# Decoder layer: hi and lo parts of two activation forms side by side, one 512-column matmul for two of 256, and reordered bank reads

## The chip, the cores and the metric

The kernel runs on one core of a Trainium2 chip. The metric is device microseconds of one execution: the median of 3 runs before is 844.3 us (843.54 to 844.47). The profiled execution, whose trace is quoted here, took 844.19 us; its span from first to last instruction is 842.4 us.

## The reference

One decoder layer on 512 tokens of width 1024, in float32. The parts that matter here:

```python
def memory_cross_attention(h, m, w_q, w_kv, w_o):
    q = (h @ w_q).reshape(b, s, MEM_HEADS, MEM_HEAD_DIM)
    kv = (m @ w_kv).reshape(b, mlen, 2, MEM_HEADS, MEM_HEAD_DIM)   # m: 256 memory tokens
    k, v = kv[:, :, 0], kv[:, :, 1]
    probs = softmax(einsum('bshd,bmhd->bhsm', q, k) / sqrt(MEM_HEAD_DIM))
    ...
# in reference():
    x = x + merged @ w_mix_out            # after attention, convolution and their merge
    x = x + memory_cross_attention(rms_norm(x, ..), rms_norm(mem, ..), ...)
    hf = rms_norm(x, norm_ffn)
    gate, up = split(hf @ w_ffn_in, 2)    # w_ffn_in: 1024 x 5632
    x = x + (silu(gate) * up) @ w_ffn_out # w_ffn_out: 2816 x 1024
return rms_norm(x, norm_final)
```

## The kernel before

**Two parts of a number.** TensorE takes operands in fp32r. Every operand is therefore split: ScalarE casts it (`hi`), and VectorE subtracts the cast from the original (`lo`, in the code the *rest*). A product is three matmuls, hi x hi, hi x lo and lo x hi, added up in one PSUM bank. A bank holds 512 float32 columns. PSUM has three pools of banks: `pmm` (2 banks), `pz` (4) and `po` (2); a bank is taken again when its last reader is done.

**Memory keys** (`km`). Eight groups, one per 128 key columns. `load_w` fetches the weights (SyncE queue), ScalarE casts them (L151), VectorE makes the rest (L152, `wl`). For each of eight k a 512-column matmul multiplies the weights' hi part with a tile `mgs[k]` that holds hi and lo of the 256 memory tokens side by side, and a 256-column matmul adds the weights' lo part times the tokens' hi part. The two halves of the bank are added afterwards: ScalarE copies the right one (L666), VectorE adds the left one (L667), then multiplies by the tokens' norm (L668) and splits the result. Groups alternate between the two banks of `pmm`. A scheduler sets the order on each engine here; `after(x, earlier)` forces an order on one engine.

**Entry.** `residual` adds the attention's result to the stream, block by block of 128 channels, and `forms_of` turns each pair of an even and an odd channel block (`xe`, `xo`) into seven activation forms of 256 columns, one half of the tokens each.

**Gate and up products.** The hidden width is cut into 22 blocks `m` of 128. For each block the gate and up weights (two column blocks), the even and odd channels and the two halves of the tokens make a 2 x 2 by 2 x 2 block product, done in seven products `i` = 0 to 6 in place of eight (in Strassen's manner). `ffn_form` makes hi and lo of a weight form (cast L872, rest L873, tile `wf`), six products ahead. `product` runs three matmuls for each of four k, 12 matmuls of 256 columns (L883). The order of all products is a list, `uses`, which interleaves block m with block m + 1. Three banks serve a block: `z` (products 0, 3, 4, 5), `v` (product 1) and `y` (products 2 and 6). They are read between products: ScalarE copies z (L904), VectorE reads v after product 1 (L906) and y after product 6 (L909), and `second` reads y after product 2 (L914) before product 6 adds onto it. `evict` multiplies by the norm (L921), applies Silu (ScalarE, L923) and forms the activations (L931, L935). `mean2` and `r2b` work out the norm of the stream during the first blocks: VectorE splits the sums of squares (L196, L197) and two matmuls average them (L202). From here to the end PE, ACT and DVE run in the order in which the code is written (`manual_schedule`).

**The end of these products** prepares the first activation forms (`f01`, `fh`) and weights (`out_cast`, its rest `rest_of`, L964) of the output products (L1152), of which 276 matmuls of 512 columns follow.

Of the kernel before, what the change touches and what calls it, by code (L numbers as in the profile page):

```python
# [44 lines left out]
def hybrid_layer(ctx: ExitStack, tc: tile.TileContext, xT_d, memT_d, mem_d, cols_d, wv_d, win_d,  # L45
# [607 lines left out]
            mem_split(m)  # L653


    km = []
    for m in range(KD):
        w = load_w(wmk_d[m])
        ps = mmtile("km")
        for k in range(KD):  # L660
            nc.tensor.matmul(ps, w[0][:, k, :], mgs[k], start=k == 0, stop=False,
                             skip_group_check=True)
            nc.tensor.matmul(ps[:, :MEM], w[1][:, k, :], mg[k][0], start=False, stop=k == KD - 1,
                             skip_group_check=True)
        t = tmp("km", MEM)
        nc.scalar.copy(t, ps[:, MEM:])  # L666
        nc.vector.tensor_tensor(out=t, in0=ps[:, :MEM], in1=t, op=ALU.add)  # L667
        nc.vector.tensor_tensor(out=t, in0=t, in1=rmb, op=ALU.mult)  # L668
        if m % 2 == 0:
            pair = unit("kmh"), unit("kml")  # L670
        hi, lo = (u[:, (m % 2) * MEM:(m % 2 + 1) * MEM] for u in pair)
        nc.scalar.copy(hi, t)
        nc.vector.tensor_tensor(out=lo, in0=t, in1=f(hi), op=ALU.subtract)
        km.append((hi, lo))
        if m == 0:
            merged.append(split(sig[0], "m"))
    vm = [[None] * 2 for _ in range(MT)]
    for n in range(2):
        pss = [ztile("vm") for _ in range(MT)]
        for c in range(4):  # L680
            w = load_w(wmv_d[n, c], 512)
            for j in range(2):
                k = 2 * c + j
                for t in range(MT):
                    sl = slice(t * P, (t + 1) * P)
                    mm3(pss[t], (mg[k][0][:, sl], mg[k][1][:, sl]),
                        (w[0][:, j, :], w[1][:, j, :]), k == 0, k == KD - 1)
        for t in range(MT):
            vm[t][n] = split(pss[t], "vm", rm[:, t:t + 1])

    def forms_of(xe, xo):

        b11, b12, b21, b22 = xe[:, :HS], xe[:, HS:], xo[:, :HS], xo[:, HS:]
        c, d = f(unit("c1")), f(unit("c2"))
        n1, t3, n2, t4 = c[:, :HS], c[:, HS:], d[:, :HS], d[:, HS:]
        nc.vector.tensor_tensor(out=n1, in0=b11, in1=b12, op=ALU.subtract)
        nc.vector.tensor_tensor(out=t3, in0=b22, in1=b12, op=ALU.subtract)
        nc.vector.scalar_tensor_tensor(out=n2, in0=n1, scalar=-1.0, in1=b22, op0=ALU.mult,  # L700
                                       op1=ALU.subtract)
        nc.vector.scalar_tensor_tensor(out=t4, in0=n2, scalar=-1.0, in1=b21, op0=ALU.mult,
                                       op1=ALU.subtract)
        u = unit("xf")
        nc.scalar.copy(u[:, :HS], b11)
        nc.vector.tensor_tensor(out=u[:, HS:], in0=b11, in1=f(u[:, :HS]), op=ALU.subtract)
        (oh, ol), (ch, cl), (dh, dl) = split(xo, "xo"), split(c, "xc"), split(d, "xd")
        a, b = slice(0, HS), slice(HS, S)
        return [(u[:, a], u[:, b]), (oh[:, a], ol[:, a]), (ch[:, a], cl[:, a]),
                (dh[:, a], dl[:, a]), (ch[:, b], cl[:, b]), (dh[:, b], dl[:, b]),  # L710
                (oh[:, b], ol[:, b])]

    def residual(w_dram, act, old, gain, pairs=False):

# [160 lines left out]

    def product(ps, m, i, ks=range(KP)):

        w = wforms[m, i]
        for k in ks:
            hi, lo = (w[:, j, k * P:(k + 1) * P] for j in range(2))  # L880
            xh, xl = x2f[k][i]
            for j, (a, b) in enumerate(((hi, xh), (hi, xl), (lo, xh))):
                nc.tensor.matmul(ps[:, :HS], a, b, start=i < 3 and k == 0 and j == 0,  # L883
                                 stop=k == KP - 1 and j == 2, skip_group_check=True)

    banks, silus = {}, []
    acts = {}

    def bank_of(m, i):
# [6 lines left out]
            banks[m]["y"] = otile("y")  # L896
        return banks[m]["zvyzzzy"[i]]

    def reads(m, i):

        b = banks[m]
        z, s, t = b["z"][:, :HS], b["s"], b["t"]
        if i in (0, 3, 4):
            nc.scalar.copy((s[:, :HS], None, None, s[:, HS:], t[:, :HS])[i], z)  # L904
        elif i == 1:
            nc.vector.tensor_tensor(out=b["g"][:, :HS], in0=b["v"][:, :HS], in1=s[:, :HS],  # L906
                                    op=ALU.add)
        elif i == 6:
            nc.vector.tensor_tensor(out=b["g"][:, HS:], in0=b["y"][:, :HS], in1=s[:, HS:],  # L909
                                    op=ALU.add)  # L910

    def second(m):
        b = banks[m]
# [165 lines left out]
    with tc.manual_schedule(engines={mybir.EngineType.PE, mybir.EngineType.Activation,  # L1079
# [6 lines left out]
        for n, (m, i) in enumerate(uses):  # L1086
# [3 lines left out]
                product(bank_of(m, i), m, i)  # L1090
            if i == 4:
                reads(m, i)
            else:
                if i == (2 if m == 1 else 1) and m > 0:
                    second(m - 1)
                reads(m, i)
            if n + AHEAD < len(uses):
# [31 lines left out]
            elif (m, i) == (NF - 1, 4):  # L1129
# [5 lines left out]
                rest_of(*x2)  # L1135
                n2_of(x2[0], 0)
        w = out_cast(*w23(1))
        evict(NF - 1, 0)
        evict(NF - 1, 1)
        rest_of(*x3)  # L1140
        rest_of(*w)
        evict(NF - 1, 2)


# [314 lines left out]
```

## Time and profile before

| | |
|---|---|
| Median of 3 runs | 844.3 us |
| Profiled execution | 844.19 us, span 842.4 us |
| TensorE (PE) busy | 833.8 us, 99% |
| Weight loads (PEld) busy | 731.0 us, 87% |
| VectorE (DVE) busy | 658.7 us, 78% |
| ScalarE (ACT) busy | 464.2 us, 55% |
| GpSimd (POOL) busy | 155.6 us, 18% |
| Matmuls | 4694 |

Busy times are shares of one span; the engines work side by side. Matmuls overlap, so a row's duration of a matmul (283 ns for 256 columns) is longer than the step from its start to the next one's. In a row, `out<-in` names the tile written and the tiles read, `L883` is the line of the kernel, and a bracket at the end gives the idle time ahead of the instruction on its engine and what ended it.

### The profile page before, as it was taken

How to read it: one execution, taken by the hardware profiler on the slowest of the kernel's cores; microseconds unless marked ns; L12 is line 12 of the kernel's file. 1: busy time of each engine (PE TensorE's matmuls, PEld its weight loads, DVE VectorE, ACT ScalarE, POOL GpSimd, SP SyncE). 2: the span in 40 equal slices, each digit the busy share in tenths (PEclk: the TensorE clock that was granted, in tenths of full speed). 3: DMA queues.
4: the chain of work that ended last, by engine and by line, in shares of the span. 5: the costliest groups of instructions: out<-in, count | busy, mean ns of one | idle time of the engine just before them, and what ended most of it. 6: DMA issues, size and time to landing. Idle time of an engine off the chain costs nothing.

```text
span 842.4 us, 12559 instructions
## 1 busy us (share of the span) xinstructions
PE 833.8 (99%) x4694; PEld 731.0 (87%) x4694; DVE 658.7 (78%) x1066; ACT 464.2 (55%) x835; POOL 155.6 (18%) x165
## 2 busy tenths in 40 slices
PE   9999999999999999999999999999999999999996
PEld 7888888888888888888888889999999999988885
DVE  7879899986756577586555679888887888899886
ACT  7567878674332255433444557655555555666654
POOL 0011131210666620173000101111111110000401
PEclk9999999999999999999999999999999999999998
DMA  8452454134687865566431425777677772465552
GB/s 301 151 168 102 120 115 114 59 116 172 244 308 269 315 231 189 187 230 238 134 80 51 113 51 153 198 184 190 178 181 194 189 181 85 150 224 202 176 186 101
DMA packets 51359, 143.73 MB, mean 171 GB/s; under 512 B 5761, under 2 KB 7041, under 8 KB 48482
## 3 DMA queue, kind: packets, MB, share of 16 engines
q1 hardware_dynamic: 41650, 107.89, 38.5%
q0 software_dynamic: 9360, 34.75, 15.8%
q8 instruction: 37, 0.61, 0.3%
q10 hardware_dynamic: 288, 0.28, 0.1%
q14 instruction: 24, 0.20, 0.1%
HBM read 125.20 MB, written 13.64 MB: 165 GB/s over the span
## 4 chain that ended last, share of the span: by engine, by line
PE 98%; DMA 1%; DVE 0%; ACT 0%; issue 0%; SPq 0%; DVEq 0%
PE z L883 15%; PE p L1152 12%; PE pr L156 8%; PE pr L157 8%; PE pr L158 8%; PE y L883 8%; PE v L883 4%; PE r L157 3%; PE r L156 3%; PE r L158 3%; PE v L284 2%; PE mq L157 2%; PE mq L158 2%; PE mq L156 2%; PE br L157 2%; PE br L156 2%
## 5 line engine op out<-in xcount | busy, mean ns | idle before, releaser
L151 ACT CAST wh<-wr 128x1024 fp32r<-128x1024 f32 x84 | 88.1, 1051 | 149.4 <-issue 83.7
L152 DVE TENSOR_TENSOR wl<-wr,wh 128x1024 fp32r<-128x1024 f32 x84 | 112.2, 1336 | 37.2 <-ACT wh L151 37.2
L156 PE MATMUL pr<-xgh,wh 128*128 128x512 f32 x288 | 112.8, 392 | 0.0
L157 PE MATMUL pr<-xgl,wh 128*128 128x512 f32 x288 | 112.3, 390 | 0.0
L158 PE MATMUL pr<-xgh,wl 128*128 128x512 f32 x288 | 112.2, 390 | 0.0
L607 POOL TENSOR_TENSOR pre<-pre 128x512 f32<-128x512 f32 x44 | 70.1, 1597 | 32.6 <-DMA pre<-in_w_ffn_out_dram 30.3
L852 POOL DMA_DIRECT2D ws<-in_w_ffn_in_dram x22 | 26.6, 1210 | 256.2 <-DVE wf L873 123.5
L883 PE MATMUL z<-xdh,wf 128*128 128x256 f32 x352 | 70.4, 283 | 0.0
L158 PEld LDWEIGHTS pr<-xgh,wl 128*128 128x128 f32 x288 | 54.1, 188 | 11.6
L156 PEld LDWEIGHTS pr<-xgh,wh 128*128 128x128 f32 x288 | 54.1, 188 | 10.6
L157 PEld LDWEIGHTS pr<-xgl,wh 128*128 128x128 f32 x288 | 54.1, 188 | 10.3
L904 ACT COPY sa<-z 128x256 f32<-128x256 f32 x44 | 16.4, 372 | 81.5 <-PE z L883 81.5
L883 PEld LDWEIGHTS z<-xdh,wf 128*128 128x128 f32 x352 | 58.0, 192 | 0.0
L873 DVE TENSOR_TENSOR wf<-s,wf 128x512 fp32r<-128x512 f32 x44 | 30.4, 690 | 25.7 <-ACT wf L872 25.3
L883 PE MATMUL z<-xdl,wf 128*128 128x256 f32 x176 | 49.8, 283 | 0.0
L964 DVE TENSOR_TENSOR wl<-wr,wh 128x1024 fp32r<-128x1024 f32 x33 | 41.0, 1242 | 4.3 <-ACT wh L1031 4.3
L1031 ACT CAST wh<-wr 128x1024 fp32r<-128x1024 f32 x33 | 34.6, 1050 | 4.4 <-DMA wr<-sums 2.1
L883 PE MATMUL y<-xch,wf 128*128 128x256 f32 x176 | 35.4, 283 | 0.0
L883 PE MATMUL v<-xoh,wf 128*128 128x256 f32 x176 | 35.4, 283 | 0.0
L883 PE MATMUL z<-xf,wf 128*128 128x256 f32 x264 | 35.4, 283 | 0.0
L883 PE MATMUL z<-xch,wf 128*128 128x256 f32 x176 | 35.3, 283 | 0.0
L883 PE MATMUL y<-xoh,wf 128*128 128x256 f32 x176 | 35.3, 283 | 0.0
(350 smaller groups left out, 2377.5 us busy)
## 6 DMA issues: line engine op xcount, KB each, us to landing
wr<-in_w_in_dram SPq DMA_DIRECT2D x36, 512.0 KB, 3.3
pre<-in_w_ffn_out_dram POOLq DMA_DIRECT2D x11, 1024.0 KB, 7.9
sums<-pre POOLq DMA_DIRECT2D x11, 1024.0 KB, 5.1
ws<-in_w_ffn_in_dram SPq DMA_DIRECT2D x22, 512.0 KB, 3.7
wg<-in_w_ffn_in_dram SPq DMA_DIRECT2D x22, 512.0 KB, 4.5
ws<-in_w_ffn_in_dram POOLq DMA_DIRECT2D x22, 512.0 KB, 6.1
wr<-sums SPq DMA_DIRECT2D x22, 512.0 KB, 3.9
wr<-in_w_ffn_out_dram SPq DMA_DIRECT2D x16, 512.0 KB, 3.9
```

Of the source, the lines that this page charges most:

```text
L151: after(nc.scalar.copy(h2, raw), lead[-1:])
L152: lows.append(nc.vector.tensor_tensor(out=l2, in0=raw, in1=f(h2), op=ALU.subtract))
L156: nc.tensor.matmul(ps, a[0], b[0], start=start, stop=False, **kw)
L157: nc.tensor.matmul(ps, a[0], b[1], start=False, stop=False, **kw)
L158: nc.tensor.matmul(ps, a[1], b[0], start=False, stop=stop, **kw)
L607: nc.gpsimd.tensor_tensor(out=t[:, a, :], in0=t[:, a, :], in1=t[:, b, :], op=ALU.add)
L852: nc.gpsimd.dma_start(s13, a[:, 0:4:3, :], accum_op=ALU.add)
L873: nc.vector.tensor_tensor(out=w[:, 1, :], in0=raw, in1=f(w[:, 0, :]), op=ALU.subtract)
L883: nc.tensor.matmul(ps[:, :HS], a, b, start=i < 3 and k == 0 and j == 0, stop=k == KP - 1 and j == 2, skip_group_check=True)
L964: nc.vector.tensor_tensor(out=lo, in0=src, in1=f(hi), op=ALU.subtract)
L1031: nc.scalar.copy(hi, raw)
L1152: nc.tensor.matmul(res[i][s2], a[:, ts], b, start=j == 0 and n == 0, stop=n == 2 and j == (BEHIND - 1 if (i, s2) == (5, 1) else NJ - 1))
```

## The change

Five edits go together.

- `forms_of` puts hi and lo of the odd block's two halves (forms 1 and 6) side by side in one 512-column tile each (`beside`). In place of one 512-column cast and one 512-column rest there are two of 256 columns; the second pair comes last.
- `product` then runs, for forms 1 and 6, four 512-column matmuls (hi weights times hi and lo side by side) and after them four 256-column matmuls (lo weights times hi): 8 matmuls, not 12. The bank's right half now holds a part of the sum, so `reads` of v and y becomes `joined_halves`: two VectorE additions, of which the second reads the first's result.
- At the entry, `second(0)` follows product (0, 4); before it followed product (1, 2). `second(1)` keeps its place after product (2, 1).
- At the end of the gate and up products the two rests (`x3` and `w`) are written ahead of `evict(NF - 1, 0)`; before they stood behind `evict(NF - 1, 1)`.
- Memory keys: the eight 512-column matmuls of a group come first, then the eight of 256; and the rest of a weight tile is ordered behind the bank read (`ready`) of the group four before it.

```diff
@@ -653,18 +653,20 @@
             mem_split(m)
 
 
-    km = []
+    km, ready = [], []
     for m in range(KD):
         w = load_w(wmk_d[m])
+        after(lows[-1], ready[m - 4:m - 3] if m > 3 else ())
         ps = mmtile("km")
         for k in range(KD):
             nc.tensor.matmul(ps, w[0][:, k, :], mgs[k], start=k == 0, stop=False,
                              skip_group_check=True)
+        for k in range(KD):
             nc.tensor.matmul(ps[:, :MEM], w[1][:, k, :], mg[k][0], start=False, stop=k == KD - 1,
                              skip_group_check=True)
         t = tmp("km", MEM)
         nc.scalar.copy(t, ps[:, MEM:])
-        nc.vector.tensor_tensor(out=t, in0=ps[:, :MEM], in1=t, op=ALU.add)
+        ready.append(nc.vector.tensor_tensor(out=t, in0=ps[:, :MEM], in1=t, op=ALU.add))
         nc.vector.tensor_tensor(out=t, in0=t, in1=rmb, op=ALU.mult)
         if m % 2 == 0:
             pair = unit("kmh"), unit("kml")
@@ -679,6 +681,8 @@
         pss = [ztile("vm") for _ in range(MT)]
         for c in range(4):
             w = load_w(wmv_d[n, c], 512)
+            if n == 0:
+                after(lows[-1], ready[c + 4:c + 5])
             for j in range(2):
                 k = 2 * c + j
                 for t in range(MT):
@@ -704,11 +708,19 @@
         u = unit("xf")
         nc.scalar.copy(u[:, :HS], b11)
         nc.vector.tensor_tensor(out=u[:, HS:], in0=b11, in1=f(u[:, :HS]), op=ALU.subtract)
-        (oh, ol), (ch, cl), (dh, dl) = split(xo, "xo"), split(c, "xc"), split(d, "xd")
         a, b = slice(0, HS), slice(HS, S)
-        return [(u[:, a], u[:, b]), (oh[:, a], ol[:, a]), (ch[:, a], cl[:, a]),
-                (dh[:, a], dl[:, a]), (ch[:, b], cl[:, b]), (dh[:, b], dl[:, b]),
-                (oh[:, b], ol[:, b])]
+
+        def beside(src, s):
+            both = unit(s)
+            nc.scalar.copy(both[:, a], src)
+            nc.vector.tensor_tensor(out=both[:, b], in0=src, in1=f(both[:, a]), op=ALU.subtract)
+            return both[:, a], both[:, b], both
+
+        first = beside(b21, "xo")
+        (ch, cl), (dh, dl) = split(c, "xc"), split(d, "xd")
+        last = beside(b22, "xo")
+        return [(u[:, a], u[:, b]), first, (ch[:, a], cl[:, a]), (dh[:, a], dl[:, a]),
+                (ch[:, b], cl[:, b]), (dh[:, b], dl[:, b]), last]
 
     def residual(w_dram, act, old, gain, pairs=False):
 
@@ -875,13 +887,23 @@
 
     def product(ps, m, i, ks=range(KP)):
 
+        rests = []
         w = wforms[m, i]
         for k in ks:
             hi, lo = (w[:, j, k * P:(k + 1) * P] for j in range(2))
-            xh, xl = x2f[k][i]
+            xh, xl, *both = x2f[k][i]
+            if both:
+                nc.tensor.matmul(ps, hi, both[0], start=i < 3 and k == 0, stop=False,
+                                 skip_group_check=True)
+                rests.append((ps[:, :HS], lo, xh))
+                continue
             for j, (a, b) in enumerate(((hi, xh), (hi, xl), (lo, xh))):
                 nc.tensor.matmul(ps[:, :HS], a, b, start=i < 3 and k == 0 and j == 0,
                                  stop=k == KP - 1 and j == 2, skip_group_check=True)
+        for operands in rests:
+            nc.tensor.matmul(*operands, start=False,
+                             stop=ks[-1] == KP - 1 and operands is rests[-1],
+                             skip_group_check=True)
 
     banks, silus = {}, []
     acts = {}
@@ -896,6 +918,10 @@
             banks[m]["y"] = otile("y")
         return banks[m]["zvyzzzy"[i]]
 
+    def joined_halves(out_, bank, old):
+        nc.vector.tensor_tensor(out=out_, in0=bank[:, :HS], in1=old, op=ALU.add)
+        nc.vector.tensor_tensor(out=out_, in0=bank[:, HS:], in1=out_, op=ALU.add)
+
     def reads(m, i):
 
         b = banks[m]
@@ -903,11 +929,9 @@
         if i in (0, 3, 4):
             nc.scalar.copy((s[:, :HS], None, None, s[:, HS:], t[:, :HS])[i], z)
         elif i == 1:
-            nc.vector.tensor_tensor(out=b["g"][:, :HS], in0=b["v"][:, :HS], in1=s[:, :HS],
-                                    op=ALU.add)
+            joined_halves(b["g"][:, :HS], b["v"], s[:, :HS])
         elif i == 6:
-            nc.vector.tensor_tensor(out=b["g"][:, HS:], in0=b["y"][:, :HS], in1=s[:, HS:],
-                                    op=ALU.add)
+            joined_halves(b["g"][:, HS:], b["y"], s[:, HS:])
 
     def second(m):
         b = banks[m]
@@ -1090,8 +1114,10 @@
                 product(bank_of(m, i), m, i)
             if i == 4:
                 reads(m, i)
+                if m == 0:
+                    second(m)
             else:
-                if i == (2 if m == 1 else 1) and m > 0:
+                if i == 1 and m > 1:
                     second(m - 1)
                 reads(m, i)
             if n + AHEAD < len(uses):
@@ -1135,10 +1161,10 @@
                 rest_of(*x2)
                 n2_of(x2[0], 0)
         w = out_cast(*w23(1))
+        rest_of(*x3)
+        rest_of(*w)
         evict(NF - 1, 0)
         evict(NF - 1, 1)
-        rest_of(*x3)
-        rest_of(*w)
         evict(NF - 1, 2)
```

VectorE in the memory keys, the first group's bank read: `wl` is the rest of a weight tile, `km` the bank and the sum, `kml` the key's rest. Before:

```order
L152 TENSOR_TENSOR wl_3021<-wr_3018,wh_3020 128x1024
L152 TENSOR_TENSOR wl_3050<-wr_3047,wh_3049 128x1024
L667 TENSOR_TENSOR km_2946<-km_2929,km_2946 128x256
L668 TENSOR_TENSOR km_2946<-km_2946,rmb 128x256
L152 TENSOR_TENSOR wl_3081<-wr_3078,wh_3080 128x1024
L673 TENSOR_TENSOR kml_2951<-km_2946,kmh_2950 128x256
L667 TENSOR_TENSOR km_2981<-km_2964,km_2981 128x256
```

After:

```order
L152 TENSOR_TENSOR wl_3021<-wr_3018,wh_3020 128x1024
L669 TENSOR_TENSOR km_2946<-km_2929,km_2946 128x256
L152 TENSOR_TENSOR wl_3050<-wr_3047,wh_3049 128x1024
L670 TENSOR_TENSOR km_2946<-km_2946,rmb 128x256
L675 TENSOR_TENSOR kml_2951<-km_2946,kmh_2950 128x256
L669 TENSOR_TENSOR km_2981<-km_2964,km_2981 128x256
L152 TENSOR_TENSOR wl_3081<-wr_3078,wh_3080 128x1024
```

The bank read (L667, now L669) has moved from behind the rest `wl_3050` to ahead of it; the multiplication and the key's rest stand ahead of the next bank read.

VectorE at the entry of the gate and up products, from block 1's read of v to the split of the sums of squares: `wf` are rests of weight forms, `sb` the result of `second(0)`, `acch` and `accl` the two parts of the sums. Before:

```order
L906 TENSOR_TENSOR fg_4870<-v_4869,sa_4804 128x256
L873 TENSOR_TENSOR wf_4884<-wg_4857,wf_4884 128x512
L873 TENSOR_TENSOR wf_4900<-ws_4743,wf_4900 128x512
L914 TENSOR_TENSOR sb_4772<-y_4793,sb_4772 128x256
L873 TENSOR_TENSOR wf_4917<-wg_4857,wf_4917 128x512
L873 TENSOR_TENSOR wf_4932<-a_4747,wf_4932 128x512
L862 TENSOR_TENSOR s_4935<-s_4837,wg_4745 128x512
L196 CAST acch_4937<-acc_4354 128x512
L197 TENSOR_TENSOR accl_4938<-acc_4354,acch_4937 128x512
```

After:

```order
L922 TENSOR_TENSOR fg_4875<-v_4874,sa_4809 128x256
L923 TENSOR_TENSOR fg_4875<-v_4874,fg_4875 128x256
L885 TENSOR_TENSOR wf_4886<-wg_4862,wf_4886 128x512
L938 TENSOR_TENSOR sb_4780<-y_4798,sb_4780 128x256
L885 TENSOR_TENSOR wf_4903<-ws_4751,wf_4903 128x512
L885 TENSOR_TENSOR wf_4919<-wg_4862,wf_4919 128x512
L885 TENSOR_TENSOR wf_4934<-a_4755,wf_4934 128x512
L874 TENSOR_TENSOR s_4937<-s_4842,wg_4753 128x512
L196 CAST acch_4939<-acc_4354 128x512
L197 TENSOR_TENSOR accl_4940<-acc_4354,acch_4939 128x512
```

The read of v has become two rows (L922, L923), as has block 0's read ahead of this piece, and `second(0)` (L914, now L938) stands one rest earlier.

VectorE at the end of the gate and up products, around the last block's read of y: `a` is a half of an activation block, `fh` and `f01l` are rests of activation forms, `wl` rests of output weights. Before:

```order
L985 SCALAR_TENSOR_TENSOR a_5324<-a_5324 128x256
L909 TENSOR_TENSOR fg_7571<-y_7591,sa_7532 128x256
L921 TENSOR_TENSOR fg_7571<-fg_7571,r0b_4988 128x512
L964 TENSOR_TENSOR fh_7715<-a_5324,fh_7715 128x256
L964 TENSOR_TENSOR wl_7733<-wr_7730,wh_7732 128x1024
L931 SCALAR_TENSOR_TENSOR a_7707<-z_7531,fg_7571 128x256
L931 SCALAR_TENSOR_TENSOR a_7708<-sb_7533,fg_7571 128x256
L964 TENSOR_TENSOR wl_7776<-wr_7773,wh_7775 128x1024
L964 TENSOR_TENSOR f01l_7780<-a_5590,f01h_7779 128x512
```

After:

```order
L1009 SCALAR_TENSOR_TENSOR a_5308<-a_5308 128x256
L922 TENSOR_TENSOR fg_7456<-y_7473,sa_7417 128x256
L923 TENSOR_TENSOR fg_7456<-y_7473,fg_7456 128x256
L988 TENSOR_TENSOR fh_7594<-a_5308,fh_7594 128x256
L988 TENSOR_TENSOR wl_7609<-wr_7606,wh_7608 128x1024
L945 TENSOR_TENSOR fg_7456<-fg_7456,r0b_4987 128x512
L955 SCALAR_TENSOR_TENSOR a_7586<-z_7416,fg_7456 128x256
L955 SCALAR_TENSOR_TENSOR a_7587<-sb_7418,fg_7456 128x256
L988 TENSOR_TENSOR wl_7652<-wr_7649,wh_7651 128x1024
L988 TENSOR_TENSOR f01l_7656<-a_5562,f01h_7655 128x512
```

The read has two rows, and the rests `fh` and `wl_7609` stand between it and the multiplication by the norm (L921, now L945), which stood ahead of them.

## The prediction

> **What bounds the kernel now.** I read the busy table of the page first, then its chain of work that ended last, then three stretches of the time windows.
>
> ```profile
> PE 833.8 (99%) x4694; PEld 731.0 (87%) x4694; DVE 658.7 (78%) x1066; ACT 464.2 (55%) x835; POOL 155.6 (18%) x165
> PE 98%; DMA 1%; DVE 0%; ACT 0%; issue 0%; SPq 0%; DVEq 0%
> 300.39:324.19 23.80, 23.66 (x131) 19.70 (x130) 18.44 (x30) 12.64 (x22) 0.66 (x2) 1.00 0.58 203
> 504.35:726.55 222.20, 222.20 (x1851) 222.11 (x1850) 185.58 (x348) 122.98 (x250) 24.52 (x22) 1.00 0.65 172
> 726.55:789.14 62.59, 62.59 (x278) 51.78 (x277) 60.03 (x94) 41.76 (x65) 0.04 (x1) 1.00 0.57 193
> ```
>
> TensorE runs 833.8 of 842.4 us and carries 98% of the chain; the granted clock is 1.00 in the three stretches (memory keys, gate and up products, output products). The windows' columns are the stretch, its length, then PE, PEld, DVE, ACT, POOL. In the second TensorE never pauses, so its time is the sum of its steps from one matmul to the next, and a change gains there only by shortening that sum, and loses where it makes TensorE wait. The last two show what stands close behind: VectorE is busy 84% of the products and 96% of the first output products. The PEld column is full too (222.11 of 222.20), but those loads overlap each other and the matmuls, so I go by steps.
>
> ```profile
> 529.43 4.32 PE z L883 x36
> 726.71 62.59 PE p L1152 x276
> ```
>
> 36 matmuls of 256 columns take 4.32 us: 120.0 ns each. 276 of 512 columns take 62.59 us: 226.8 ns each. Twice 120.0 is 240.0, so 13.2 ns are saved whenever two narrow ones become one wide one, whatever part of a matmul that fixed cost is.
>
> **The change, part by part.**
>
> *Wide matmuls in two of seven products.* Each of 22 blocks has forms 1 and 6; in each, for four k, the pair hi x hi and hi x lo becomes one 512-column matmul: 22 x 2 x 4 = 176 pairs, 176 x 13.2 ns = 2.32 us off TensorE, all on the path. The memory keys below show what a change of width costs when it alternates (about 6 ns a pair); here width changes once per product, 44 x 6 ns = 0.26 us at most. I take 2.32 and keep 2.06 as the other end.
>
> The Trainium skill, "TensorE: Matmul & The Clock Gate", section "Back-to-back issue gap", gives a warm step of N/2.4 + 2.5 ns. By it a pair would save 2.5 ns and the whole 0.44 us; the two rows above give a fixed part of 13 ns in this stage, so the trace does not agree and the sum goes by the trace.
>
> *Memory keys: 512-column matmuls first, bank read earlier.*
>
> ```profile
> 303.33 1.05 ACT L151 CAST wh<-wr 128x1024 fp32r<-128x1024 f32 x1 [1.87 <-PE km L661]
> 304.28 0.37 ACT L666 COPY km<-km 128x256 f32<-128x256 f32 x1
> 304.41 1.23 DVE L152 TENSOR_TENSOR wl<-wr,wh 128x1024 fp32r<-128x1024 f32 x1 [1.27 <-ACT wh L151]
> 305.56 0.42 DVE L667 TENSOR_TENSOR km<-km,km 128x256 f32<-128x256 f32 x1
> 306.01 0.42 DVE L668 TENSOR_TENSOR km<-km,rmb 128x256 f32<-128x256 f32 x1
> 308.73 0.42 DVE L667 TENSOR_TENSOR km<-km,km 128x256 f32<-128x256 f32 x1
> 308.79 0.28 PE L663 MATMUL km<-mg,wl 128*128 128x256 f32 x1
> 309.19 0.50 PE L661 MATMUL km<-mg,wh 128*128 128x512 f32 x1
> 309.53 0.27 PE L663 MATMUL km<-mg,wl 128*128 128x256 f32 x1
> ```
>
> The second group's bank read (L667) ends at 308.73 + 0.42 = 309.15 and TensorE's next group starts at 309.19: the two banks rotate, and the read was late behind a 1.23 us subtraction (304.41, then L667 at 305.56). The matmul after such a wait steps 0.34 us (309.19 to 309.53) instead of 0.23, so a release costs about 0.15 us beyond the reader's end. I use that below. The stage is 23.80 us with one foreign 512-column matmul: 23.57 for 64 pairs, where 64 x (226.8 + 120.0) ns = 22.20. All of it recovered is 1.37 us: about 1.0 in waits, 0.36 in alternating widths.
>
> Does the reordered VectorE queue recover it? Now the read stands ahead of the subtraction. The wide matmuls, first, free the cast's buffer 0.96 us (8 x 120 ns) earlier, so the cast of 303.33 starts near 302.4, the copy of L666 follows the group's end at 303.35, and the read ends near 304.1, not 305.98. Group two begins at 305.9: 1.8 us spare. Later groups have a spare of 1.4 by the same steps (cast 1.05, copy 0.37, read 0.42). The subtraction is moved behind, but its result is first used eight wide matmuls into its group, four loads later. I take 1.37; the low end is 0.36, all waits left.
>
> *Bank reads become two.* Each joined read is two 256-column additions, the second reading the first's result. L668 reads L667's result and starts 0.45 us after it, so 44 reads add 44 x 0.45 = 19.8 us of VectorE, 0.9 a block.
>
> ```profile
> 550.36:560.44 10.08, 10.08 (x86) 10.08 (x85) 8.04 (x16) 5.33 (x11) 1.20 (x1) 1.00 0.70 187
> POOL ws L852 <- DVE wf L873: 123.5, 14, 9.0
> ws<-in_w_ffn_in_dram POOLq DMA_DIRECT2D x22, 512.0 KB, 6.1
> 510.75:519.68 8.93, 8.93 (x76) 8.93 (x76) 8.81 (x18) 5.16 (x11) 1.21 (x1) 1.00 0.65 177
> 519.60:526.85 7.25, 7.25 (x61) 7.16 (x60) 7.09 (x14) 5.64 (x11) 1.74 (x2) 1.00 0.85 232
> ```
>
> A steady block has 8.04 of 10.08 us busy; 8.94 of the new 9.97 still fits, so I charge nothing there: the 1.0 us left idle is the cover, and without it each block would pay its excess. Nor do I charge the loads: no DMA is added or moved past another, but the accumulating one (POOL, issued when VectorE frees its buffer, landed 6.1 us later) can be issued up to 0.9 us later; three blocks' buffers are in flight, so it serves a use more than half a block of 10 us after it lands. If that cover were gone, ScalarE's casts would wait by as much. At the entry there is no cover: 8.81 of 8.93, then 7.09 of 7.25.
>
> *Entry.* The four 512-column splits of the odd half become eight of 256 on ScalarE and VectorE: two short ones for one long, under 0.1 us a pair, and the last waits in VectorE's gap before L906. Nothing charged. What follows is a queue that only grows.
>
> ```profile
> 510.75 0.42 DVE L906 TENSOR_TENSOR fg<-v,sa 128x256 f32<-128x256 f32 x1
> 515.20 0.68 DVE L873 TENSOR_TENSOR wf<-wg,wf 128x512 fp32r<-128x512 f32 x1
> 515.80 0.68 DVE L873 TENSOR_TENSOR wf<-ws,wf 128x512 fp32r<-128x512 f32 x1
> 516.40 0.42 DVE L914 TENSOR_TENSOR sb<-y,sb 128x256 f32<-128x256 f32 x1
> 517.30 0.28 PE L883 MATMUL y<-xoh,wf 128*128 128x256 f32 x1
> 518.99 0.69 DVE L197 TENSOR_TENSOR accl<-acc,acch 128x512 fp32r<-128x512 f32 x1
> 520.42 0.40 PE L202 MATMUL varb<-accl,mean_r 128*128 128x512 f32 x1
> 526.43 0.42 DVE L914 TENSOR_TENSOR sb<-y,sb 128x256 f32<-128x256 f32 x1
> 527.83 0.28 PE L883 MATMUL y<-xoh,wf 128*128 128x256 f32 x1
> ```
>
> Two joined reads (L906 of blocks 0 and 1) stand ahead of L197: its end moves from 519.68 to 520.58. TensorE wants that result at 520.42, less three joined products (3 x 0.053): 520.26. With the release it goes on at 520.73, 0.47 late. The first L914 comes 0.90 later too, but is moved ahead of one 512-column subtraction (0.60 from start to start: 515.20, 515.80), so it starts at 516.70 and ends at 517.12; TensorE wants it at 517.30 less two joined products, 517.19: just in time, or 0.1 late. The second L914 has three joined reads ahead, 1.35 less 0.2 of gaps: it ends at 528.0, released 528.15, and TensorE, 0.47 late, arrives at 528.09. So the entry costs 0.5 us, not the sum of both waits. Ends: 0 (the backlog is absorbed) and 0.9 (both waits in full).
>
> *The end's rests.*
>
> ```profile
> 730.89 0.42 DVE L985 SCALAR_TENSOR_TENSOR a<-a 128x256 f32<-128x256 f32 x1
> 731.35 0.41 ACT L968 CAST fh<-a 128x256 fp32r<-128x256 f32 x1 [2.92 <-DVE a L985]
> 731.66 1.05 ACT L1031 CAST wh<-wr 128x1024 fp32r<-128x1024 f32 x1
> 732.47 0.62 PE L1152 MATMUL p<-wh,fh 128*128 128x512 f32 x2
> 732.61 0.62 ACT L923 ACTIVATE fg<-fg 128x512 f32<-128x512 f32 x1
> 732.74 1.23 DVE L964 TENSOR_TENSOR wl<-wr,wh 128x1024 fp32r<-128x1024 f32 x1
> 734.29 0.39 PE L1152 MATMUL p<-wl,fh 128*128 128x512 f32 x1
> 735.68 0.69 DVE L964 TENSOR_TENSOR f01l<-a,f01h 128x512 fp32r<-128x512 f32 x1
> 737.91 0.39 PE L1152 MATMUL p<-wh,f01l 128*128 128x512 f32 x1
> ```
>
> Times here are against the start of the output products. L985 comes 0.55 later: 0.45 for the joined read of block 20, and 0.1 because two joined products stand between VectorE's last idle gap and the end, which come sooner by 2 x 0.053. That is 731.44. Block 21's joined read then ends at 732.65 for a matmul due at 732.70 (the second of the pair at 732.47), 0.1 late. The rest (wl at 732.74) needs its cast, which stands on ScalarE behind a short one that waits for L985: 731.86 + 0.04 + 0.31 (731.35 to 731.66) + 1.05 = 733.26, so it runs 733.30 to 734.53, and the matmul of 734.29 goes at 734.68. Behind it now come the multiplication (0.69), the Silu (0.63, ScalarE waits in it), the next cast (1.05), its rest (1.23) and f01l (0.69): 738.6, released 738.76, against 737.91. In place of the wait that the earlier rests avoid, the moved Silu holds every cast queued behind it. Cost 0.85 us, again the latest, not the sum. Before, f01l ended at 736.37, 1.5 us early, so the low end is 0; a queue that stays late through stretch three, 96% busy, gives the high end, 1.7, twice my cost.
>
> *Sum.* -2.32 - 1.37 + 0.50 + 0.85 = -2.3 us against the profiled execution's 844.19 (span 842.4 and 1.8 around it): 841.9. The median of the runs, 844.3, is 0.1 above; I say 841.9.
>
> **The rivals.**
>
> 1. *VectorE's lateness is absorbed.* For it: each waiting spot had 0.5 to 1.5 us in hand, and I charge every joined read in full; against: the entry windows show 2% idle. Then -2.32 - 1.37 = -3.7 and 840.6.
> 2. *Lateness is carried.* The output products have 60.03 of 62.59 us busy on VectorE, so a queue 1.6 us late meets TensorE again block after block. Entry 0.9 and end 1.7 give -1.1: 843.2, within 0.2% (1.7 us, about what a measurement of this kernel can tell from no change).
> 3. *The fixed cost is not saved*: a wide matmul here takes two narrow ones' time. Against it, the 226.8 ns row, from the same data type. Then -1.37 + 1.35: 844.2. The rule cited above from the Trainium skill ("TensorE: Matmul & The Clock Gate", "Back-to-back issue gap") points this way, with 0.44 us for the step instead of none.
> 4. *Slower: VectorE bounds the products.* If its idle 2.04 us a block are waits that cannot shrink, in its in-order queue behind ScalarE's casts and TensorE's results, a block takes 10.08 + 0.90 and not 9.97: 20 blocks x 0.9 = 18 us, near 861. It decides once more than 1.03 us (9.97 - 8.94) a block must stay idle. Against: the form rests are made several products ahead, so a wait there can be made up.
>
> **How the numbers follow.** My sum 0.58, rival 1 0.21, rival 2 0.14, rival 3 0.03, rival 4 0.04. The sum's own range is 841.0 to 842.8, of which 0.02 lies above 842.6 (-0.2%). Faster 0.56 + 0.21 = 0.77; same 0.02 + 0.14 + 0.03 = 0.19; slower 0.04. The range 840.4 to 843.3 reaches from rival 1 to rival 2, a little beyond each, and leaves out rivals 3 and 4 and some of the edges; the memory keys at their low end, 842.9, and the wide matmuls at theirs, 842.2, lie inside.
>
> **What would show it.** Of the changed kernel: 4 wide and 4 narrow matmuls of a joined product near 1.39 us; a steady block near 9.97 us; the memory keys near 22.4 us with no wait for the bank read; one wait of about half a microsecond at the second matmul of the mean, and waits at the first output products. If the steady block stays at 10.08, the first term is wrong; if the waits are missing, the last two.

## Result and the profile after

| | before | changed |
|---|---|---|
| Median | 843.77 us (843.21 to 844.47, 17 runs) | 842.37 us (842.04 to 843.04, 17 runs) |
| Profiled execution's span | 842.4 us | 840.6 us |
| TensorE busy, matmuls | 833.8 us, 4694 | 831.9 us, 4518 |
| VectorE busy | 658.7 us | 673.3 us |

The changed kernel takes 0.9982 of the time before (95% interval 0.9976 to 0.9988), 1.4 us less. Compared once more, on the chip of the last experiments, it took 0.9986 (0.9977 to 0.9995). The forecast was 841.9 us in a range of 840.4 to 843.3: the time lies in it, 0.5 us on the slow side. One execution of both_moved below (2706.82 us) and one of sums_on_pool (3910.42 us, the one that was profiled) took over three times as long as the others of the same kernel and are left out of the ratios.

From the page of the changed kernel, the busy table and the chain of work that ended last:

```profile
PE 831.9 (99%) x4518; PEld 721.3 (86%) x4518; DVE 673.3 (80%) x1114; ACT 464.9 (55%) x839; POOL 155.7 (19%) x165
PE 96%; DVE 2%; ACT 1%; issue 0%; DVEq 0%; ACTq 0%
```

TensorE still sets the time, but the chain now lies on VectorE and ScalarE for 3% of the span, where before neither came to one per cent. The time windows of the three stages shown before, memory keys, gate and up products and output products up to the final transposes, and a steady block (the block that took 10.08 us):

```profile
299.99:322.31 22.32, 22.32 (x130) 19.65 (x129) 18.21 (x31) 13.46 (x23) 0.58 (x1) 1.00 0.59 213
502.55:723.65 221.10, 220.76 (x1676) 212.52 (x1675) 201.30 (x391) 123.07 (x251) 24.68 (x22) 1.00 0.65 172
723.65:787.23 63.58, 63.48 (x279) 51.40 (x277) 60.41 (x95) 41.75 (x65) 0.00 (x0) 1.00 0.55 187
548.16:558.15 9.99, 9.99 (x79) 9.64 (x78) 9.17 (x19) 5.30 (x11) 1.20 (x1) 1.00 0.67 185
```

The products are 1.10 us shorter, the output products 0.99 us longer. The keys' window no longer holds the one foreign 512-column matmul (it now stands in the next stage); of the 1.48 us by which the window is shorter, 0.23 is that matmul's step, so the keys gained 23.57 - 22.32 = 1.25 us. In the products TensorE is busy 220.76 of 221.10 us; before it never paused there. With 0.09 us after the output products that is -1.25 - 1.10 + 0.99 + 0.09 = -1.3 us, and the runs measured -1.4. The stages ahead of the keys and between the keys and the products vary by some tenths between executions and are left out of it.

Where TensorE waits, from the waits of its weight loads in the changed kernel (in total, times, longest):

```profile
PEld p L1178 <- DVE wl L988: 0.5, 2, 0.4
PEld varb L202 <- DVE accl L197: 0.5, 1, 0.5
...
PEld p L1178 <- DVE f01l L988: 0.4, 1, 0.4
PEld z L901 <- ACT sb L930: 0.4, 1, 0.4
...
PEld xt L1263 <- DVE uv L1188: 0.4, 1, 0.4
```

No wait of `km` is left. The mean waits for `accl`, the first output products for `wl` and `f01l`, as the forecast said; the wait of `z` for ScalarE's copy `sb` it had not named. These columns count a load's idle time; what a wait costs is read from the steps of the matmuls. At the mean, and at product (1, 5):

```profile
518.09 0.69 DVE L197 TENSOR_TENSOR accl<-acc,acch 128x512 fp32r<-128x512 f32 x1
518.30 0.40 PE L202 MATMUL varb<-acch,mean_r 128*128 128x512 f32 x1
518.83 0.50 PE L202 MATMUL varb<-accl,mean_r 128*128 128x512 f32 x1
519.17 1.60 PE L901 MATMUL z<-xf,wf 128*128 128x256 f32 x12
...
522.61 0.69 DVE L129 SCALAR_TENSOR_TENSOR ra<-ra,rv 128x512 f32<-128x512 f32 x1
522.98 0.63 PE L904 MATMUL v<-xo,wf 128*128 128x256 f32 x4
523.39 0.37 ACT L930 COPY sb<-z 128x256 f32<-128x256 f32 x1 [1.69 <-DVE ra L129]
523.81 0.39 PE L901 MATMUL z<-xdh,wf 128*128 128x256 f32 x1 [0.20 <-ACT sb L930]
```

The mean's second matmul steps off 0.53 us after the first and the next one 0.34 us after it, where 0.23 is normal: 0.41 us. Four narrow matmuls from 522.98 would end at 523.45; product (1, 5) starts at 523.81, 0.36 late, and its first step is 0.23 us where 0.12 is normal, so 0.47 us are lost. ScalarE had stood idle for 1.69 us when the copy that empties the bank was let go by L129, a step of the norm; the product that the copy reads had ended at about 522.2 us, so 1.2 us of this are a wait for L129. The copy's destination is a buffer that L129 had read. VectorE had reached L129 late because its queue has no gap there. The same wait stands in the trace before:

```profile
524.07 0.37 ACT L904 COPY sb<-z 128x256 f32<-128x256 f32 x1 [0.76 <-DVE ra L129]
```

There the copy ended at 524.44 and product (1, 5) began at 524.95, so TensorE lost nothing by the wait: half a microsecond was in hand.

The end, VectorE, ScalarE and the matmul that waits longest:

```profile
729.67 0.42 DVE L988 TENSOR_TENSOR fh<-a,fh 128x256 fp32r<-128x256 f32 x1
730.38 1.22 DVE L988 TENSOR_TENSOR wl<-wr,wh 128x1024 fp32r<-128x1024 f32 x1 [0.29 <-ACT wh L1055]
731.52 0.68 DVE L945 TENSOR_TENSOR fg<-fg,r0b 128x512 f32<-128x512 f32 x1
732.24 0.63 ACT L947 ACTIVATE fg<-fg 128x512 f32<-128x512 f32 x1 [1.89 <-DVE fg L945]
733.84 1.23 DVE L988 TENSOR_TENSOR wl<-wr,wh 128x1024 fp32r<-128x1024 f32 x1 [0.18 <-ACT wh L1055]
734.99 0.68 DVE L988 TENSOR_TENSOR f01l<-a,f01h 128x512 fp32r<-128x512 f32 x1
735.72 0.50 PE L1178 MATMUL p<-wh,f01l 128*128 128x512 f32 x1
```

This is the chain that the forecast wrote out: multiplication, Silu, cast, rest, `f01l`, and TensorE waiting for the last of them. From the start of the output products, `f01l` ends after 12.02 us; the forecast had 12.05.

### The profile page after: what moved, and what is told of

It is laid out like the page before. It is cut to its first block, busy times and chain, and to the rows that moved or that the text cites. A ratio compares the mean times of both kernels' runs of the same rounds, so it can differ in the third digit from the quotient of the medians.

```text
span 840.6 us, 12271 instructions
## 1 busy us (share of the span) xinstructions
PE 831.9 (99%) x4518; PEld 721.3 (86%) x4518; DVE 673.3 (80%) x1114; ACT 464.9 (55%) x839; POOL 155.7 (19%) x165
## 4 chain that ended last, share of the span: by engine, by line
PE 96%; DVE 2%; ACT 1%; issue 0%; DVEq 0%; ACTq 0%
PE z L901 14%; PE p L1178 11%; PE pr L156 8%; PE pr L157 8%; PE pr L158 8%; PE y L901 4%; PE r L158 3%; PE r L157 3%; PE r L156 3%; PE v L284 3%; PE y L896 2%; PE v L896 2%; PE km L662 2%; PE mq L158 2%; PE mq L157 2%; PE mq L156 2%
## 5 line engine op out<-in xcount | busy, mean ns | idle before, releaser
L152 DVE TENSOR_TENSOR wl<-wr,wh 128x1024 fp32r<-128x1024 f32 x84 | 110.7, 1317 | 31.8 <-ACT wh L151 31.7
L988 DVE TENSOR_TENSOR wl<-wr,wh 128x1024 fp32r<-128x1024 f32 x33 | 40.4, 1223 | 4.9 <-ACT wh L1055 4.2
L901 PEld LDWEIGHTS z<-xf,wf 128*128 128x128 f32 x264 | 33.5, 192 | 0.1
L901 PEld LDWEIGHTS z<-xdl,wf 128*128 128x128 f32 x176 | 33.5, 190 | 0.0
```

What stands on the lines that cost most here:

```text
L152: lows.append(nc.vector.tensor_tensor(out=l2, in0=raw, in1=f(h2), op=ALU.subtract))
L988: nc.vector.tensor_tensor(out=lo, in0=src, in1=f(hi), op=ALU.subtract)
```

## Experiments

**Theory.** Each part acts by itself. The keys give 1.25 us; a joined product gives less than 4 x 13.2 ns, since a change of width costs TensorE something; the doubled bank reads make VectorE late in two places where it has no gap, and TensorE waits there for about 0.9 and 1.0 us. The rivals are in the expectations. "Products" and "output products" are the second and third window above.

**km_only**: the kernel before with the memory keys' hunks of the diff alone.

> The kernel before with the memory keys' edit alone. Theory A (each part of the change acts by itself, as the trace after reads): the memory keys and values stages of the trace after are 1.24 us shorter than before, nothing else moves: -1.2 us, 842.5 against 843.8. Theory B (the forecast's own term): -1.37 us. Theory C (the keys' time is only handed on to a wait further down, and the products bring the whole gain): no change, 843.8. C differs from the other two by 1.2 us; A and B are too close for the times, the stage's length in the trace tells them apart.

842.86 us against 843.84, ratio 0.9987 (0.9978 to 0.9996). Its windows:

```profile
300.29:322.61 22.32, 22.32 (x130) 19.65 (x128) 18.21 (x31) 13.46 (x23) 0.58 (x1) 1.00 0.62 216
502.80:725.00 222.20, 222.20 (x1851) 222.11 (x1850) 185.63 (x348) 122.92 (x250) 24.59 (x22) 1.00 0.66 172
725.00:787.59 62.59, 62.59 (x278) 51.76 (x277) 60.04 (x94) 41.76 (x65) 0.00 (x0) 1.00 0.59 193
```

The keys' stage is the changed kernel's to the hundredth, the other two are those of before (222.20 and 62.59). Theory A holds, C falls, and the stage tells A's 1.25 us from B's 1.37.

**products_only**: the changed kernel with those hunks undone.

> The changed kernel with the memory keys as before: wide matmuls, joined reads, the early second(0) and the early rests at the end. Theory A (trace after): a joined product with the narrow one behind it takes 2.834 us in place of 2.880, 44 of them -2.02 us; waits +0.91 us in the gate and up products and about +1.0 us at the output products: -0.1 us, 843.7 against 843.8. Theory B (the forecast's terms): -2.32 + 0.50 + 0.85 = -1.0 us, 842.8.

843.83 us against 843.84, ratio 0.9998 (0.999 to 1.0007): theory A's 843.7, not B's 842.8.

```profile
504.11:725.21 221.10, 220.76 (x1675) 212.51 (x1674) 201.21 (x391) 123.01 (x251) 24.92 (x22) 1.00 0.65 172
725.21:788.79 63.58, 63.48 (x279) 51.41 (x277) 60.41 (x95) 41.80 (x65) 0.00 (x0) 1.00 0.57 188
```

Here, too, the stages are the changed kernel's. The wide products, the subject of the change, bring nothing that can be measured in whole runs: of 1.10 us gained in one stage 0.99 are lost in the next and 0.08 behind it. All that the change gains is the memory keys.

**one_read**: the second addition is taken away, so that a part of the sum is left out.

```diff
 def joined_halves(out_, bank, old):
     nc.vector.tensor_tensor(out=out_, in0=bank[:, :HS], in1=old, op=ALU.add)
-    nc.vector.tensor_tensor(out=out_, in0=bank[:, HS:], in1=out_, op=ALU.add)
```

> The changed kernel without the second addition of each joined read (the bank's right half, the hi x lo part of the two forms, is left out of the sums); all else as in the change, the reorderings too. Theory A (VectorE's 44 dependent additions make all the new waits): no wait at the mean, at product (1, 5) and at the first output products, -1.24 - 2.02 = -3.3 us, 840.5. Theory D (the reorderings make the waits, not the additions): they stay, 842.4 as the changed kernel. Under the forecast's 13.2 ns a pair it would be -3.6, 840.2.

841.54 us, ratio 0.9971 (0.9959 to 0.9982): the time lies half-way between A's 840.5 and D's 842.4, and the stages tell why. Its windows of the products and output products, and the waits that it has at the latter:

```profile
502.66:722.83 220.17, 220.17 (x1675) 212.40 (x1674) 185.28 (x349) 122.85 (x251) 24.64 (x22) 1.00 0.66 173
722.83:785.96 63.13, 63.05 (x279) 51.54 (x277) 59.65 (x93) 41.78 (x65) 0.00 (x0) 1.00 0.58 190
```

```profile
PEld p L1177 <- DVE f01l L987: 0.4, 1, 0.4
PEld xt L1262 <- DVE uv L1187: 0.4, 1, 0.4
```

In the products theory A holds: no pause is left and the stage is 222.20 - 220.17 = 2.03 us shorter, which is what the wide matmuls give; the 0.93 us up to the changed kernel's 221.10 are the reads'. At the output products A fell half-way: 63.13, not 62.59. The wait for `f01l` stays without a single added addition, so 0.54 us come without them: from the order at the end, as theory D had it. That TensorE, made faster by the wide products, reaches the end sooner may have a small part in it; with two reads in the old order it is 0.1 us (63.35 in rests_late, where products are wide, against 63.25 in narrow_two).

**narrow_two**: the reverse. The kernel before with its narrow matmuls, and a second, dependent addition behind each read.

```diff
             nc.vector.tensor_tensor(out=b["g"][:, :HS], in0=b["v"][:, :HS], in1=s[:, :HS],
                                     op=ALU.add)
+            nc.vector.tensor_tensor(out=b["g"][:, :HS], in0=b["v"][:, :HS], in1=b["g"][:, :HS],
+                                    op=ALU.add)
 (and the same behind the read of y)
```

> The kernel before, its matmuls of 256 columns, its memory keys and its order untouched, with a second VectorE addition behind each read of v and y that takes the first one's result (it adds the sum to itself: the activations are not the layer's). Theory A (the waits come from VectorE's 44 additions and nothing else): the gate and up products + 0.9 us (223.1), the output products + 0.76 us as with the rests late (63.35). Theory M (VectorE had the time, and the waits come from the wide products, which bring TensorE to its waits sooner): within 0.3 us of 222.2 and of 62.6.

845.33 us in one run, against 844.25. Products and output products:

```profile
504.13:727.12 222.99, 222.65 (x1851) 222.19 (x1850) 201.49 (x390) 123.08 (x250) 24.66 (x22) 1.00 0.66 171
727.12:790.37 63.25, 62.94 (x279) 51.62 (x278) 60.82 (x96) 41.87 (x65) 0.00 (x0) 1.00 0.58 191
```

+0.79 and +0.66 us, near A's 0.9 and 0.76, far from M's nothing: the additions alone make TensorE wait, also where every product is narrow.

**all_wide**: why a pair saves less than 13.2 ns.

```diff
-                rests.append((ps[:, :HS], lo, xh))
+                rests.append((ps, lo, both[0]))
```

> The changed kernel with the four narrow matmuls of a joined product made 512 columns wide too (a lo x lo part is added to the right half), so that such a product is eight 512-column matmuls. Theory E (a change of width costs the time: steps are uneven only where 512 and 256 columns meet): 8 x 226.7 = 1.81 us a joined product, the steps 226 or 227 ns inside it, +18 us in all. Theory F (the 512-column step is 232.7 ns here whatever stands beside it, from the operands or the other engines' traffic): 8 x 232.7 = 1.86 us, +20 us in all.

860.48 us in one run, +18.1 us on the changed kernel's 842.37. A joined product of each kernel on TensorE, and the start of the one behind it, first the changed kernel, then this one:

```profile
592.42 1.09 PE L896 MATMUL v<-xo,wf 128*128 128x512 f32 x4
593.35 0.63 PE L904 MATMUL v<-xo,wf 128*128 128x256 f32 x4
593.82 0.28 PE L901 MATMUL z<-xdh,wf 128*128 128x256 f32 x1
```

```profile
599.59 1.09 PE L896 MATMUL v<-xo,wf 128*128 128x512 f32 x4
600.52 1.07 PE L904 MATMUL v<-xo,wf 128*128 128x512 f32 x4
601.43 0.28 PE L901 MATMUL z<-xdh,wf 128*128 128x256 f32 x1
```

In both the first four wide matmuls take 0.93 us, 232 ns each. The second four take 0.91 us here. From start to start, as means over 43 products (the first one is run in two pieces at the entry), the eight steps are 233, 236, 228, 232, 231 and then 226.7 three times. So neither theory is right as it stood: the operands and the stage do not set 232.7 ns (F), and no return to narrow matmuls is needed for the uneven steps (E). They belong to the first five wide matmuls behind a narrow one. Part of it comes back: the four narrow ones behind them and the next product take 471 and 1432.5 ns where 480 and 1440 are the rule. In the changed kernel a joined product and the narrow one behind it take 1400.8 + 1432.5 = 2833.3 ns in place of 2880: 46.7 ns, 11.7 a pair, and 44 of them 2.05 us.

**alternating**: wide and narrow matmuls in turn, k by k.

```diff
+                nc.tensor.matmul(ps[:, :HS], lo, xh, start=False, stop=k == KP - 1,
+                                 skip_group_check=True)
-                rests.append((ps[:, :HS], lo, xh))
 (and the loop over rests is gone)
```

> The changed kernel with wide and narrow matmuls in turn inside a joined product (k by k), not the four wide ones first. Theory K (each change of width from narrow to wide costs some 6 ns net): three more changes in each of 44 products, 44 x 3 x 6 = 0.8 us more in the gate and up products, 221.9 us; the memory keys of before ran so, 353 ns a pair where nothing waited. Theory L (one transient per product, whatever the order in it): 221.1.

The window of its products:

```profile
502.66:724.28 221.62, 221.27 (x1675) 212.70 (x1674) 201.27 (x391) 123.10 (x251) 24.91 (x22) 1.00 0.66 172
```

+0.52 us, between K (+0.8) and L (none): 12 ns a product, 4 for each further change of width. Putting the wide ones first, as the change does, is worth that half microsecond.

**mean_early**: the two places of the mean moved.

```diff
-            if (m, i) == (0, 5):
+            if (m, i) == (1, 2):
                 mean2 = mean2()
-            elif (m, i) == (1, 3):
+            elif (m, i) == (0, 6):
```

> The changed kernel with the split of the sums of squares (L196, L197) written one product earlier, behind product (1, 2), and the mean's two matmuls with the four VectorE steps of the norm behind product (0, 6), not (1, 3). Theory A (at the entry VectorE's queue has no gap, so the two joined reads delay L197 and the norm's chain, and TensorE meets both): the split ends about 1.2 us earlier, the norm's steps about 1.3 us, no wait at the mean and none at product (1, 5): the gate and up products 221.10 - 0.9 = 220.2 us. Theory G (the queue is only late in another place): the steps moved back, second(0) or the weight forms' rests, make TensorE wait as long, 221.1.

The products' window, and the mean on TensorE and VectorE:

```profile
502.26:723.12 220.86, 220.69 (x1675) 212.53 (x1674) 201.28 (x391) 123.13 (x251) 24.56 (x22) 1.00 0.66 173
```

```profile
516.59 0.69 DVE L197 TENSOR_TENSOR accl<-acc,acch 128x512 fp32r<-128x512 f32 x1
516.71 0.47 PE L202 MATMUL varb<-acch,mean_r 128*128 128x512 f32 x1
517.34 0.50 PE L202 MATMUL varb<-accl,mean_r 128*128 128x512 f32 x1 [0.17 <-DVE accl L197]
```

The stage is 0.24 us shorter than the changed kernel's, where A hoped for 0.9. TensorE's wait for `sb` is gone, as A said: the norm's chain did cause it. The wait at the mean is not, and there my expectation was careless: the mean's matmuls moved ahead by a product (518.30 to 516.71), the split by as much (518.09 to 516.59), so nothing changed between them.

**silu_early** and **rests_late**: two other orders at the end.

```diff
 silu_early:                       rests_late:
  rest_of(*x3)                     -rest_of(*x3)
 -rest_of(*w)                      -rest_of(*w)
  evict(NF - 1, 0)                  evict(NF - 1, 0)
  evict(NF - 1, 1)                  evict(NF - 1, 1)
 +rest_of(*w)                      +rest_of(*x3)
  evict(NF - 1, 2)                 +rest_of(*w)
                                    evict(NF - 1, 2)
```

> The changed kernel with one line moved at the end: the rest of the weights (w) stands behind evict(NF - 1, 0) and (NF - 1, 1), the rest x3 stays ahead. Theory A (of the 0.99 us that the first output products lost, the moved Silu with the cast, rest and f01l behind it makes some 0.5 us, the joined read the remainder): the multiplication starts 1.5 us earlier, the Silu and the cast behind it about 1.4 us, the two late waits (0.5 us of steps) go, the weight rest comes 0.24 us later: the stretch is 63.58 - 0.25 = 63.3 us. Theory H (the Silu does not matter, VectorE's sum of work does): 63.6.

> The changed kernel with the end in the order of before: both rests behind evict(NF - 1, 0) and (NF - 1, 1). Theory A: the activation's rest ends 0.6 us later and TensorE waits for it, the Silu's chain is early: the waits change place, not size, 63.5 us (63.2 to 63.9). Theory I (the early rests are what saves the end, the joined read would cost more without them): 64.2 us or more. Theory J (the early rests cost the 0.54 us that stay with single reads, where the stretch is 63.13 against 62.59): 63.0 us.

The output products of the first, then of the second, with the wait that each has there in place of the three:

```profile
723.85:787.07 63.22, 63.07 (x279) 51.60 (x278) 60.79 (x96) 41.97 (x65) 0.00 (x0) 1.00 0.58 191
...
PEld p L1178 <- DVE wl L988: 0.6, 1, 0.6
```

```profile
723.96:787.31 63.35, 63.08 (x279) 51.61 (x278) 60.89 (x96) 41.95 (x65) 0.00 (x0) 1.00 0.58 192
...
PEld p L1178 <- DVE wl L988: 0.7, 1, 0.7
```

63.22 is theory A's 63.3, and H (63.6) falls. 63.35 lies in A's range, and I (64.2 or more) and J (63.0) fall, though the change's own order is 0.23 us worse than the old one. With joined reads the old order costs 63.35 - 62.59 = 0.76 us, the change's 0.99, the one between 0.63.

**both_moved**: both places in one kernel.

```diff
-            if (m, i) == (0, 5):
+            if (m, i) == (0, 4):
                 mean2 = mean2()
-            elif (m, i) == (1, 3):
+            elif (m, i) == (0, 6):
...
                 n2_of(x2[0], 1)
+                w = out_cast(*w23(1))
                 x3 = half_form(3, 1, 0)
...
-        w = out_cast(*w23(1))
         rest_of(*x3)
```

> The changed kernel with two moves. Entry: the split of the sums of squares written two products earlier than in the change, behind second(0) after product (0, 4), the mean and the norm behind product (0, 6): with the mean one product earlier its split has to come two earlier. End: the cast of the weights w23(1) on ScalarE ahead of that of x3, where ScalarE stands idle 2.9 us and the load has landed (issued 722.22, 4.0 us); the rests then follow in the change's order. Theory A (VectorE's queue order alone makes the waits): gate and up products 222.21 - 2.05 = 220.2 us with no wait at the mean or at product (1, 5); at the end wl starts 0.36 us earlier (730.02, not 730.38), the Silu and f01l as much: waits of 0.1 to 0.3 us are left, 62.8 us (62.6 to 63.1). With the memory keys that is -1.25 - 2.05 + 0.2 = -3.1 us against the kernel before: 840.7 against 843.8. Theory G (lateness only moves on): 221.1 and 63.6 us, 842.4.

841.85 us against 844.25, ratio 0.9971 (0.996 to 0.9982). Its products and output products together are the shortest of the complete kernels, 283.99 us.

```profile
502.68:723.48 220.80, 220.80 (x1676) 212.65 (x1674) 201.25 (x391) 123.24 (x251) 24.95 (x22) 1.00 0.67 173
723.48:786.67 63.19, 63.19 (x279) 51.48 (x277) 60.31 (x95) 41.79 (x65) 0.00 (x0) 1.00 0.58 189
```

Theory A hoped for 220.2 and 62.8. Against the kernel before, the 2.4 us gained lie between A's 3.1 and G's 1.4. At the end 0.39 of the 0.99 us come back. The wait at the mean is gone, but 220.80 - 220.17 = 0.63 us is still paid, in eight small delays between 515 and 534 us of 0.02 to 0.14 us each. Theory G is mostly right at the entry: a queue without a gap hands its lateness on, and a better order recovers only a third of it (0.3 of 0.93).

**sums_on_pool**: both_moved with two sums of weight forms taken off VectorE, and **changed_again** beside it.

```diff
-                ffn_raw(*uses[n + AHEAD + SUM_AHEAD])
+                ffn_raw(*uses[n + AHEAD + SUM_AHEAD], nc.gpsimd if n in (8, 9) else nc.vector)
```

> The kernel of both_moved with the two sums of weight forms that stand in VectorE's queue at 518.2 and 520.2 us (L874, 0.6 us each from start to start) on GpSimd, which is idle between two DMA issues there and took 1.29 us for such a sum at 480.7. Theory A (the entry is short of VectorE time: the order only shares the lateness out, less work takes it away): 1.2 us less queue by 520.9, the eight small waits that both_moved keeps between 515 and 536 us (0.6 us in all) go: gate and up products 220.2 us, not 220.8, and 841.3 in all. Theory N (the waits left come from ScalarE's or the norm's chain): 220.8, 841.9.

> The changed kernel once more, beside the one above on one chip: 842.4 us, 1.1 us behind it by theory A, 0.5 by theory N.

844.07 us against 844.02 for the kernel before (ratio 1.0, 0.9991 to 1.0009) and 843.07 for the changed kernel beside it: neither theory's time, 2.8 us above A's, and 1.0 us longer than the changed kernel where A had it 1.1 us shorter. No trace of a usual execution was kept, so where the time went is not known. That GpSimd's sums came too late for the weight forms would fit, but it is not shown, and stays open.

## Why the forecast was right, and where it was not

- **Memory keys**, forecast -1.37, measured -1.25. The reordered queue takes all waits away, as worked out. The other 0.12 us is the change of width from group to group, which was not charged here: the first group follows 512-column matmuls and takes 2.77 us, the seven others follow 256-column ones and take 2.79 each.
- **Wide matmuls**, forecast -2.32, measured -2.05. The forecast wrote down 2.06 as the other end, by 6 ns for each product's change of width, and took 2.32. The term mis-sized is this one: the 6 ns should have been charged. That the fixed part of a step is about 13 ns here and not 2.5, on which the trace and the Trainium skill's "TensorE: Matmul & The Clock Gate", section "Back-to-back issue gap", differed, is borne out: by 2.5 ns a pair the products would have gained 0.44 us. That section gives the 2.5 ns for the gap of an isolated matmul and says that the spacing in a stream of weight loads and matmuls, as here, is set by both, which the forecast did not say.
- **Steady blocks**, charged with nothing: 9.99 us against the forecast 9.97, so VectorE's cover held; rival 4 would have had 10.98.
- **Entry waits**, forecast +0.50, measured +0.93. The wait at the mean came as written (0.41 against 0.47). The step that failed is the list of the entry's waits, and with it the sentence that the entry costs the latest of them and not their sum. Of the two that the forecast weighed, the second one, the later bank read `second(1)`, held TensorE up nowhere, so that reading held. But a wait that was not in the list added 0.47 us (0.36 and the longer step behind it): the norm's chain on VectorE and ScalarE's copy into a buffer which that chain holds. I followed the split and `second`, and not the four steps of the norm behind the mean. The forecast's high end for the entry, 0.9, had the size, for another reason.
- **End waits**, forecast +0.85, measured +0.99, and 0.09 behind them. The chain was right row by row: Silu, cast, rest, `f01l`. What was not said is that the moved rests avoid less than the moved Silu costs: the old order would have cost 0.76. Nor was it said that 0.54 us would be there without the joined reads, with which the forecast's chain began (one_read).
- **Rivals.** Absorption (840.6) did not happen: every term of lateness came, so the time went from the likeliest case towards rival 2 (843.2). The fixed cost was saved, so rival 3 falls.

The errors all have one sign: 0.12 + 0.27 + 0.43 + 0.14 + 0.09 = 1.05 us, between the sum of -2.3 and the -1.3 of the stages. The forecast's time is only 0.5 us off, and that is in part luck: it was reckoned from 844.2 us, and the median of 17 runs before is 843.77. As a gain, 2.3 us were forecast and 1.4 measured. That is under 0.2%, the line that the forecast drew between faster and the same: it had given 0.77 to a larger gain, and 0.19 to a time this close.

## What to carry to other kernels

The change shortened one engine's stream by a fixed part per instruction, and paid the other engine's price in the places without a gap, not in the steady state. Before such a change, look for the stretches where the second engine is busy 98% and add up all ways on which its lateness reaches the first, buffers that come free included. Moving work within such a queue returned 0.3 of 0.93 us; less work in it returned all, but in a kernel that leaves a part of the sum out (one_read), and moving work to GpSimd did not pay. Measure the parts of a combined edit apart: here a reorder of eight groups earned the whole 1.3 us, and the edit that gave the change its name earned nothing that the runs can tell.

## What the runs showed of the hardware that was not expected

- Behind 256-column matmuls the first five of 512 columns step 233, 236, 228, 232 and 231 ns, and 226.7 from the sixth on. In all_wide it is the same in 43 products to within a nanosecond, whatever the other engines did beside them, which speaks against contention. The changed kernel's memory keys show it in seven of eight groups, all but the one that follows 512-column matmuls. In the products, net of the shorter narrow steps behind, it costs 6.5 ns a product (2833.3 ns against 4 x 226.7 + 16 x 120).
- Stages of kernels that share an edit mostly agree to 0.02 us (the keys 22.32 in ten profiles; unedited, with their waits, 23.77 to 23.91), while whole runs of one kernel spread by about a microsecond. One profile of a stage told more here than the times of eleven runs.
